# A hybrid encoder layer in float32 on one core: the seven products of the paired down projection in another order, kept sums added later, the gate activation in one call

## The chip, the cores and the metric

The kernel runs on one core of one Trainium2 chip. Its time is the device time of one execution in microseconds (us); lower is better. The time of the kernel before is given as the median of three runs. Beside them stands one profiled execution, from which every duration below is taken.

The engines are named as the profile names them: PE multiplies matrices (PEld is its weight load), DVE (vector), ACT (scalar, activation functions) and POOL (GpSimd) work element by element, SP only issues DMA transfers. ACT and POOL issue some transfers too. SPq is the transfer queue of SP.

## The reference

One layer is applied to two request groups, 256 and 512 tokens of width 1024, all in float32. Three token mixers (a state-space scan, a differential attention and an attention into memory tokens) are gated, merged and projected. The change lies in the last part, the feed-forward network (FFN):

```python
D_FF = -(-8 * D_MODEL // (3 * 256)) * 256          # 2816
    h2 = rmsnorm(x, ffn_norm_g[li])
    g, up = jnp.split(h2 @ w_gate_up[li], 2, axis=-1)
    x = x + (jax.nn.silu(g) * up) @ w_down[li]
```

## The kernel before, in words

**Products.** A float32 product is made of three matmuls: each operand is split into a high part, rounded to the type that PE takes at full speed, and a low part, the rest; high × high, high × low and low × high are summed in PSUM (lines 805 to 807 of `mm3`). The high part is one ACT operation, the low part one DVE subtraction, and the second needs the first.

**The FFN in blocks.** The 768 tokens of both groups are done together. D_FF is cut into 11 blocks of 256 hidden units. For each block there are a gate block and an up block (`block`), from block 1 on each made of seven products of half-size matrices in place of eight (a Strassen–Winograd scheme): four sums of the weights are made on POOL (`_split_w`, lines 581 to 588; each instruction of 128x512), their splits on ACT and DVE (lines 566 and 567), and DVE adds the products in PSUM up into `fs` (line 1514). A block's gate values go to `act_in` (`fa` in the profile) through `fin_gate`: ACT computes t = tanh(c/2) (line 1469), DVE (t + 1) · c (line 1470), which is twice the silu; `fin_up` multiplies the up values in (line 1474). The factor 2 is taken out where these values are split: `left` scales by 0.5.

**The paired down projection.** Blocks 1 and 2, 3 and 4, 5 and 6, 7 and 8 are each taken together after the second block's up (`down_pair`; the text calls this a pair). With A the hidden values (rows: blocks; columns: tokens 0 to 383 and 384 to 767) and B the rows of w_down (columns 0 to 511 and 512 to 1023), the pair is again seven products: A11·B11, S3·T3, S2·T2, A12·B21, S1·T1, A22·T4, S4·B22, in this order, each of 18 matmuls of 128x512 (three token tiles, two steps of k, three matmuls). The left operands A11, A12, A22 are values of `fa`, S1 to S4 are sums on DVE (`left_sum`, tiles `ls`); `left` splits them (ACT line 1552, DVE line 1553; tiles `lS2h`, `lS2l` and so on). The right operands B11, B21, B22 are weights as loaded, T1 to T4 are differences of weights: a tile `wt…x` or `wt…z` is set to a negated one by ACT (`minus`, line 604) and a transfer issued by POOL adds another piece of w_down to it in its memory (`add`, line 603). T3, T2 and T4 are made one after the other in the same tile x: T2 = T3 + B11, T4 = B21 − T2, so T4's transfer waits until T2 is split and negated. `_right` splits each (lines 595 and 596; tiles `wh68_T2`, `wl68_T2`, where 68 is the number of the weight; the profile leaves it out).

**What becomes of the products.** Four of the seven are added by DVE into the rows of the result kept on the chip (`into`, line 1577, tiles `x1` or `x`). The other three, A11·B11, S2·T2 and S1·T1 (`keep` of "1", "6" and "5"), are used by several quarters of the result: ACT copies them out of PSUM (`de`, line 1611), a transfer brings them to DRAM (line 1612), and from the second pair on a transfer issued by POOL adds them to the running sum `p_sum` there (line 1614). `down_sums` reads the three sums back at the end (SP) and adds them with 21 DVE additions (line 1654). It is called before the gate block 9. Blocks 9 and 10 go through `down_last`, plain products, whose results are stored. A product uses three PSUM banks, two of a ring of five and one of a ring of three.

**What sets the order.** Each engine runs its instructions strictly in its own order and waits for other engines by semaphores. A scheduler, which simulates the engines, chooses this order from the program and its dependencies; only transfers in `keep_in_program_order` are pinned to the order of the source. The raw weights come through a ring of three buffers `wr` (half a weight, 512 KB, issued by SP at line 547): the next half can be loaded when the oldest has been split. The split weights lie in rings of four.

Of the kernel before, what the change touches and what calls it, by code (L numbers as in the profile page):

```python
# [507 lines left out]
class WStream:  # L508
# [90 lines left out]
    def _split_d(self, i, h, kind):  # L599
# [6 lines left out]
        if kind == "d" and h == 0:  # L606
            self._right(i, "B11", r)
            self.z = new("z")
            minus(self.z, r)
            add(self.z, b12)  # L610
        elif kind == "d":
            self.x = new("x")
            minus(self.x, r)
            add(self.x, b22)
            self._right(i, "T3", self.x)
        elif h == 0:
            add(self.x, b11)
            self._right(i, "T2", self.x)
            self._right(i, "B21", r)
            self._right(i, "T1", self.z)  # L620
        else:
            minus(self.x, self.x)
            add(self.x, b21)
            self._right(i, "T4", self.x)
            self._right(i, "B22", r)
# [47 lines left out]
def hybrid_block(ctx, tc, A, outs, consts):  # L673
# [792 lines left out]
    def fin_gate(fb, c, m, cs):  # L1466
        n = cs.stop - cs.start
        t = ft_.tile([128, 512], F32, name=uid("ft"), tag="ft")
        act.activation(t[:, 0:n], c, AF.Tanh, scale=0.5)
        v.scalar_tensor_tensor(out=act_in[fb][:, m, cs], in0=t[:, 0:n], scalar=1.0, in1=c, op0=add, op1=mul)  # L1470

    def fin_up(fb, c, m, cs):
        o = act_in[fb][:, m, cs]
        v.tensor_tensor(out=o, in0=o, in1=c, op=mul)
        if fb == 0:
            hh, hl = hid[0]
            act.activation(hh[:, m, cs], o, AF.Copy, scale=0.5)
            v.scalar_tensor_tensor(out=hl[:, m, cs], in0=o, scalar=0.5, in1=hh[:, m, cs].bitcast(F32),
                                   op0=mul, op1=sub)
# [69 lines left out]
    def left(key, src):  # L1549

        hi, lo = (lf.tile([128, 2, HT], F32R, name=uid(f"l{key}{w}"), tag="l" + w) for w in "hl")
        act.activation(hi, src, AF.Copy, scale=0.5)
        v.scalar_tensor_tensor(out=lo, in0=src, scalar=0.5, in1=hi.bitcast(F32), op0=mul, op1=sub)
# [3 lines left out]
    def left_sum(o, x, y, op):  # L1557
        if o is None:
            o = stg.tile([128, 2, HT], F32, name=uid("ls"), tag="brr")
# [3 lines left out]
    def down_begin(fb):  # L1563
# [3 lines left out]
        if fb < NFB - 2:  # L1567
            left("S3", left_sum(None, a[:, :, 0:HT], a[:, :, HT:TOK], sub))
# [22 lines left out]
    def down_pair(fb):  # L1591
# [25 lines left out]
        s1 = left_sum(None, a21, a22, add)  # L1617
        s2 = left_sum(None, s1, a11, sub)
        left("S2", s2)
        into(1, 1, prod("S3", "T3"))  # L1620
        left("A12", a12)
        keep("6", prod("S2", "T2"))
        left("S1", s1)
        into(0, 0, prod("A12", "B21"))
        left("A22", a22)
        keep("5", prod("S1", "T1"))
        left("S4", left_sum(s2, a12, s2, sub))
        into(1, 0, prod("A22", "T4"))
        into(0, 1, prod("S4", "B22"))

    def down_last(fb):
# [3 lines left out]
        for r in range(2):  # L1635
            h = slice(HT * r, HT * r + HT)
            x = [L.pop("A11") if r == 0 else left("A21", a[:, :, h]), left("A2", b[:, :, h])]
            ps = [banks(), banks()]
# [7 lines left out]
    def down_sums():  # L1646

        for t in range(3):
            e = {}
            for key in "165":  # L1650
                e[key] = ft_.tile([128, 512], F32, name=uid("de"), tag="ft")
                nc.sync.dma_start(e[key], p_sum[key][:, t])
            b = {(r, c): out_block(r, c, t) for r in range(2) for c in range(2)}
            plus = lambda o, y: v.tensor_tensor(out=o, in0=o, in1=y, op=add)  # L1654
            plus(b[0, 0], e["1"])
            plus(e["6"], e["1"])
            plus(b[1, 1], e["6"])
            plus(b[1, 0], b[1, 1])
            plus(b[1, 1], e["5"])
            plus(e["6"], e["5"])  # L1660
            plus(b[0, 1], e["6"])
# [214 lines left out]
    for fb in range(1, NFB):  # L1876
        block("gate", fb)
        if fb == NFB - 2:
            down_sums()
# [55 lines left out]
```

## Time and profile before

| | us |
|---|---|
| median of 3 runs (lowest, highest) | 1785.61 (1784.14, 1787.73) |
| the profiled execution's own time | 1783.92 |
| its span, first to last instruction | 1782.1 |
| PE busy in it | 1749.7 (98%) |
| DVE busy | 1309.0 (73%) |
| ACT busy | 910.7 (51%) |
| POOL busy | 251.7 (14%) |

The FFN's first pair begins at 1381.31 us of the span, the last product ends near 1778. In rows of the profile, an instruction in order of time stands as: start, duration, engine, line, operation, output<-inputs, shape; in brackets the idle time of the engine just before it and what ended that. A row of a group has the number of instructions, the busy us, the mean ns, and the idle time before them with what ended most of it. A row of the list of waits is an engine's operation, what it waited for, and then the total us, the number of times and the longest. In tile names the running number is left out, so `wh_T` stands for the high part of T1, T2, T3 or T4.

### The profile page before, as it was taken

The page shows a single profiled execution, that of the slowest core. Times are in us where ns is not written, and L with a number is a line of the kernel's source. Part 1 is how long each engine was busy: PE and PEld are TensorE (multiplying, and loading weights), DVE is VectorE, ACT ScalarE, POOL GpSimd, SP SyncE. Part 2 cuts the span into 40 slices and gives each one's busy share as a digit, 9 for nine tenths or more (in the row PEclk, how much of TensorE's full clock was granted, in tenths as well). Part 3 has the DMA queues.
Part 4 walks back from the last instruction along what each step waited for, and adds up shares of the span by engine and source line. Part 5 has one row for each costly group of instructions (what it writes and reads, how often), then busy time and mean ns, then how long its engine had stood idle before and what let it go on. Part 6 is the DMA issues. An engine that isn't in the chain of part 4 may idle for free. (4 is left out here: it accounts for less than half of the span.)

```text
span 1782.1 us, 29580 instructions
## 1 busy us (share of the span) xinstructions
PE 1749.7 (98%) x11221; PEld 1612.2 (90%) x11221; DVE 1309.0 (73%) x2431; ACT 910.7 (51%) x1894; POOL 251.7 (14%) x283
## 2 busy tenths in 40 slices
PE   8999999999999999999989999999999999999999
PEld 8999988999999998999979888888889898989887
DVE  6665659699999579778875545452699777978795
ACT  6444434877676367778756333232334544444431
POOL 0000000000000101011110101000113333333330
PEclk9999999999999999999999999999999999999999
DMA  7223745664665477454862635332314447474742
GB/s 261 76 84 104 136 113 126 166 166 116 150 151 147 126 182 184 107 113 100 174 165 79 212 122 165 115 100 66 83 48 108 134 109 175 119 174 123 174 128 83
DMA packets 211437, 234.62 MB, mean 132 GB/s; under 512 B 59224, under 2 KB 169056, under 8 KB 211296
## 3 DMA queue, kind: packets, MB, share of 16 engines
q1 hardware_dynamic: 177872, 149.11, 28.4%
q0 software_dynamic: 27088, 71.05, 19.7%
q10 hardware_dynamic: 6336, 12.59, 1.9%
q8 instruction: 88, 1.44, 0.3%
q14 instruction: 53, 0.43, 0.1%
HBM read 163.42 MB, written 49.09 MB: 119 GB/s over the span
## 5 line engine op out<-in xcount | busy, mean ns | idle before, releaser
L641 ACT ACTIVATE wh<-wr 128x1024 fp32r<-128x1024 f32 x130 | 146.6, 1128 | 73.0 <-PE br L806 26.4
L647 DVE TENSOR_TENSOR wl<-wr,wh 128x1024 fp32r<-128x1024 f32 x84 | 110.8, 1320 | 84.1 <-ACT wh L641 82.4
L805 PE MATMUL gl<-Hhi,wh 128*128 128x256 f32 (+1 forms) x384 | 132.3, 344 | 0.0
L807 PE MATMUL gl<-Hhi,wl 128*128 128x256 f32 (+1 forms) x384 | 128.9, 336 | 0.0
L806 PE MATMUL gl<-Hlo,wh 128*128 128x256 f32 (+1 forms) x384 | 128.6, 335 | 0.0
L645 POOL DMA_DIRECT2D wl<-wr x46 | 40.2, 875 | 517.7 <-ACT wl L644 499.7
L805 PE MATMUL qk<-wh,Hhi 128*128 128x256 f32 x384 | 108.6, 283 | 1.6 <-ACT qksq L1232 1.6
L806 PE MATMUL qk<-wl,Hhi 128*128 128x256 f32 x384 | 108.6, 283 | 0.0
L807 PE MATMUL qk<-wh,Hlo 128*128 128x256 f32 x384 | 108.5, 283 | 0.0
L807 PEld LDWEIGHTS gl<-Hhi,wl 128*128 128x128 f32 x384 | 72.0, 188 | 8.0
L806 PEld LDWEIGHTS gl<-Hlo,wh 128*128 128x128 f32 x384 | 72.2, 188 | 7.2
L805 PEld LDWEIGHTS gl<-Hhi,wh 128*128 128x128 f32 x384 | 72.3, 188 | 7.0
L1332 DVE TENSOR_REDUCE nm<-sc 128x1 f32<-128x512 f32 (+1 forms) x96 | 57.1, 597 | 26.6 <-PE sc L1327 25.3
L805 PEld LDWEIGHTS qk<-wh,Hhi 128*128 128x128 f32 x384 | 73.2, 191 | 2.5 <-ACT qksq L1232 1.8
L807 PEld LDWEIGHTS qk<-wh,Hlo 128*128 128x128 f32 x384 | 73.1, 190 | 0.7
L806 PEld LDWEIGHTS qk<-wl,Hhi 128*128 128x128 f32 x384 | 73.1, 190 | 0.5
L567 DVE TENSOR_TENSOR wl_S<-ws,wh_S 128x512 fp32r<-128x512 f32 x70 | 60.5, 884 | 13.5 <-ACT wh_S L566 11.7
L566 ACT ACTIVATE wh_S<-ws 128x512 fp32r<-128x512 f32 x70 | 41.4, 624 | 55.7 <-POOL ws L588 30.4
L1334 ACT ACTIVATE p<-sc,nm 128x512 f32<-128x512 f32 (+1 forms) x96 | 59.0, 616 | 12.5 <-DVE nm L1332 12.0
L1684 ACT ACTIVATE glr<-glr 128x768 f32<-128x768 f32 x24 | 20.3, 846 | 66.2 <-DMA glr<-gl_scr 66.2
L805 PE MATMUL v<-wh,Hhi 128*128 128x256 f32 x192 | 54.1, 282 | 0.0
L806 PE MATMUL v<-wl,Hhi 128*128 128x256 f32 x192 | 54.0, 281 | 0.0
(593 smaller groups left out, 6198.2 us busy)
## 6 DMA issues: line engine op xcount, KB each, us to landing
wr<-in_w_in_dram SPq DMA_DIRECT2D x48, 512.0 KB, 5.1
wl<-wr POOLq DMA_DIRECT2D x46, 512.0 KB, 5.2
wr<-in_w_gate_up_dram SPq DMA_DIRECT2D x44, 512.0 KB, 4.5
wr<-in_w_branch_dram SPq DMA_DIRECT2D x24, 512.0 KB, 4.4
wr<-in_w_down_dram SPq DMA_DIRECT2D x22, 512.0 KB, 4.6
glr<-gl_scr POOLq DMA_DIRECT2D x24, 384.0 KB, 3.6
wr<-in_w_mem_kv_dram SPq DMA_DIRECT2D x16, 512.0 KB, 4.0
wr<-in_w_in_dram SPq DMA_DIRECT2D x32, 256.0 KB, 4.9
```

Of the source, the lines that this page charges most:

```text
L566: self.nc.scalar.activation(f(hi), src, AF.Copy)
L567: self.nc.vector.tensor_tensor(out=f(lo), in0=src, in1=f(hi).bitcast(F32), op=ALU.subtract)
L641: self.nc.scalar.activation(hi, r, AF.Copy)
L645: self.nc.gpsimd.dma_start(lo, r.bitcast(F32R), accum_op=ALU.add)
L647: self.sub.tensor_tensor(out=lo, in0=r, in1=hi.bitcast(F32), op=ALU.subtract)
L805: pe.matmul(ps, wh, xh, start=start, stop=False)
L806: pe.matmul(ps, wh, xl, start=False, stop=False)
L807: pe.matmul(ps, wl, xh, start=False, stop=stop)
L1332: v.tensor_reduce(out=nm[:, m : m + 1], in_=ps, axis=AX.X, op=ALU.max, negate=True)
L1334: act.activation(pm[:, 0:n], ps, AF.Exp, bias=nm[:, m : m + 1], accum_out=s1s[:, tt : tt + 1] if m == 0 else s2)
L1684: act.activation(g, g, AF.Tanh, scale=0.5)
```

## The change

1. The pair's products come in the order A11·B11, S3·T3, A12·B21, S4·B22, S2·T2, S1·T1, A22·T4, and so `keep` of "6" and "5" comes fifth and sixth. The right operands are split in the order B11, T3, B21, T2, B22, T1, T4 (before: B11, T3, T2, B21, T1, T4, B22); T2's negation and T4's transfer are written right after T2's split, before B22 and T1.
2. The sum S4 is written early and has a buffer of its own (tag "do"); before, it was written into S2's buffer.
3. `down_sums` is cut in three, one part for each token tile: the first is called after gate block 10, the two others inside `down_last`, behind its first splits. Its reads are pinned to program order on SP.
4. The gate activation is one ACT operation, Silu, into `act_in`. The values no longer carry the factor 2, and `left` and `fin_up` split without the factor 0.5 (`split_evac`, an existing helper: ACT line 798, DVE line 799). DVE has 2311 instructions where it had 2355 (40 gate operations of 128x384 and four smaller ones are gone), ACT one more (a table load), POOL 263 where it had 259.

```diff
         elif h == 0:
             add(self.x, b11)
+            self._right(i, "B21", r)
+        else:
             self._right(i, "T2", self.x)
-            self._right(i, "B21", r)
-            self._right(i, "T1", self.z)
-        else:
             minus(self.x, self.x)
             add(self.x, b21)
+            self._right(i, "B22", r)
+            self._right(i, "T1", self.z)
             self._right(i, "T4", self.x)
-            self._right(i, "B22", r)
...
     def fin_gate(fb, c, m, cs):
-        n = cs.stop - cs.start
-        t = ft_.tile([128, 512], F32, name=uid("ft"), tag="ft")
-        act.activation(t[:, 0:n], c, AF.Tanh, scale=0.5)
-        v.scalar_tensor_tensor(out=act_in[fb][:, m, cs], in0=t[:, 0:n], scalar=1.0, in1=c, op0=add, op1=mul)
+        act.activation(act_in[fb][:, m, cs], c, AF.Silu)
...
-        act.activation(hi, src, AF.Copy, scale=0.5)
-        v.scalar_tensor_tensor(out=lo, in0=src, scalar=0.5, in1=hi.bitcast(F32), op0=mul, op1=sub)
+        split_evac(hi, lo, src)
...
         keep("1", prod("A11", "B11"))
-        s1 = left_sum(None, a21, a22, add)
-        s2 = left_sum(None, s1, a11, sub)
+        left("A12", a12)
+        s1 = left_sum(a21, a22, add)
+        s2 = left_sum(s1, a11, sub)
+        left("S4", left_sum(a12, s2, sub, "do", 1))
+        into(1, 1, prod("S3", "T3"))
         left("S2", s2)
-        into(1, 1, prod("S3", "T3"))
-        left("A12", a12)
+        into(0, 0, prod("A12", "B21"))
+        left("S1", s1)
+        into(0, 1, prod("S4", "B22"))
+        left("A22", a22)
         keep("6", prod("S2", "T2"))
-        left("S1", s1)
-        into(0, 0, prod("A12", "B21"))
-        left("A22", a22)
         keep("5", prod("S1", "T1"))
-        left("S4", left_sum(s2, a12, s2, sub))
         into(1, 0, prod("A22", "T4"))
-        into(0, 1, prod("S4", "B22"))
...
             x = [L.pop("A11") if r == 0 else left("A21", a[:, :, h]), left("A2", b[:, :, h])]
+            if r == 0:
+                down_sums(1)
+                down_sums(2)
...
         block("gate", fb)
-        if fb == NFB - 2:
-            down_sums()
+        if fb == NFB - 1:
+            down_sums(0)
```

How the scheduler's order differs is shown at three places. The first is ACT in the first pair, from the split of T3 (weights 67 and 68 are those of w_down for blocks 1 and 2). `de` are copies of a kept product, `lS2h`, `lA12h` high parts of left operands, `wt67x` the tile of T3, T2 and T4. Before:

```order
L595 ACTIVATE wh67_T3_15496<-wt67x_15493 128x1024
L595 ACTIVATE wh68_T2_15593<-wt67x_15493 128x1024
L595 ACTIVATE wh68_B21_15597<-wr68_0_15356 128x1024
L604 ACTIVATE wt67x_15493<-wt67x_15493 128x1024
L1611 ACTIVATE de_1647_15689<-dn_1644_15668 128x512
L1612 DMA p_sum1_172<-de_1647_15689 128x512
L1611 ACTIVATE de_1648_15692<-dn_1645_15669 128x512
L1612 DMA p_sum1_172<-de_1648_15692 128x512
L595 ACTIVATE wh68_T1_15601<-wt67z_15488 128x1024
L1611 ACTIVATE de_1649_15695<-dn_1646_15670 128x512
L1552 ACTIVATE lS2h_1652_15702<-ls_1651_15700 128x768
```

And of the changed kernel:

```order
L595 ACTIVATE wh67_T3_15472<-wt67x_15469 128x1024
L595 ACTIVATE wh68_B21_15569<-wr68_0_15340 128x1024
L595 ACTIVATE wh68_T2_15575<-wt67x_15469 128x1024
L1604 ACTIVATE de_1635_15665<-dn_1632_15644 128x512
L1605 DMA p_sum1_172<-de_1635_15665 128x512
L1604 ACTIVATE de_1636_15668<-dn_1633_15645 128x512
L604 ACTIVATE wt67x_15469<-wt67x_15469 128x1024
L1605 DMA p_sum1_172<-de_1636_15668 128x512
L798 ACTIVATE lA12h_1638_15674<-fa_1608_15309 128x768
```

The split of B21 now stands ahead of that of T2, and the third product's left operand (now A12) comes five instructions and issues after T2's split, where the third one's before (S2) came nine after it. On DVE the same pair has, behind T2's low part, these rows in the changed kernel (`fs` and `fa` are the up block's sums and the hidden values, `ls` the sums of left operands; before, the low parts of B21 and T1 and the additions of an `into` stood there ahead of S2's low part):

```order
L596 TENSOR_TENSOR wl68_T2_15576<-wt67x_15469,wh68_T2_15575 128x1024
L1471 TENSOR_TENSOR fa_1608_15309<-fa_1608_15309,fs_1624_15479 128x384
L1553 TENSOR_TENSOR ls_1641_15680<-ls_1640_15678,fa_1589_15032 128x768
L1553 TENSOR_TENSOR ls_1642_15682<-fa_1608_15309,ls_1641_15680 128x768
L799 TENSOR_TENSOR lA12l_1639_15675<-fa_1608_15309,lA12h_1638_15674 128x768
```

Here the low part of A12 stands four places behind that of T2, with the sums for S2 and S4 between them.

The second place is POOL in the second pair (weights 73 and 74), from the transfer for T1 on. `wt73x<-in_w_down` are the transfers for T3, T2 and T4 in this order, `ws75…` the sums for the next gate block's weight. Before:

```order
L603 DMA wt73z_16324<-in_w_down_dram 128x2x512
L603 DMA wt73x_16329<-in_w_down_dram 128x2x512
L588 TENSOR_TENSOR ws723_16172<-wr72_1_16025,ws721_16170 128x512
L603 DMA wt73x_16329<-in_w_down_dram 128x2x512 x2
L1614 DMA p_sum1_172<-p_scr_1740_16525 128x512
L581 TENSOR_TENSOR ws750_16476<-wr75_0_16336,wr75_1_16441 128x512
```

Of the changed kernel:

```order
L603 DMA wt73z_16285<-in_w_down_dram 128x2x512
L603 DMA wt73x_16290<-in_w_down_dram 128x2x512
L588 TENSOR_TENSOR ws723_16141<-wr72_1_15994,ws721_16139 128x512
L603 DMA wt73x_16290<-in_w_down_dram 128x2x512
L581 TENSOR_TENSOR ws750_16437<-wr75_0_16297,wr75_1_16394 128x512
L582 TENSOR_TENSOR ws751_16438<-ws750_16437,wr75_0_16297 128x512
L586 TENSOR_TENSOR ws752_16439<-wr75_0_16297 128x512
L1607 DMA p_sum1_172<-p_scr_1721_16486 128x512
L603 DMA wt73x_16290<-in_w_down_dram 128x2x512
```

T4's transfer, the last row, stood right behind T2's; it now stands behind three sums of the next weight and one transfer of a kept product.

The third place is DVE at the end of the program. Before, the last of the 21 additions stood in the gate block 10, ahead of its last two gate operations:

```order
L1654 TENSOR_TENSOR x1_5_12337<-x1_5_12337,de_1996_18599 128x512
L1654 TENSOR_TENSOR x1_2_12334<-x1_2_12334,de_1995_18597 128x512
L647 TENSOR_TENSOR wl91_1_18904<-wr91_1_18748,wh91_1_18903 128x1024
L1470 SCALAR_TENSOR_TENSOR fa_2006_18747<-ft_2017_18873,fs_2007_18780 128x384
L1470 SCALAR_TENSOR_TENSOR fa_2006_18747<-ft_2019_18890,fs_2008_18781 128x384
```

Of the changed kernel (`dn` is a product of the last projection, `x1_0` to `x1_5` rows of the result, `de` the sums that were read back):

```order
L1570 TENSOR_TENSOR x1_0_12332<-x1_0_12332,dn_1993_18940 128x512
L1650 TENSOR_TENSOR x1_5_12337<-x1_5_12337 128x512
L1650 TENSOR_TENSOR de_1991_18929<-de_1991_18929,de_1992_18931 128x512
L1570 TENSOR_TENSOR x1_1_12333<-x1_1_12333,dn_1994_18941 128x512
L1570 TENSOR_TENSOR x1_2_12334<-x1_2_12334,dn_1995_18942 128x512
L1650 TENSOR_TENSOR x1_5_12337<-x1_5_12337,de_1992_18931 128x512
L1650 TENSOR_TENSOR x1_2_12334<-x1_2_12334,de_1991_18929 128x512
```

The last additions of kept sums now stand between the additions that take the last projection's products out of PSUM; the first seven stand in the up block 10.

More of the change, by code (lines that the diff above doesn't have):

```diff
@@ L1476, in fin_up @@
             hh, hl = hid[0]
-            act.activation(hh[:, m, cs], o, AF.Copy, scale=0.5)
-            v.scalar_tensor_tensor(out=hl[:, m, cs], in0=o, scalar=0.5, in1=hh[:, m, cs].bitcast(F32),
-                                   op0=mul, op1=sub)
+            split_evac(hh[:, m, cs], hl[:, m, cs], o)
     def new_block(what, fb):
@@ L1551, in left, with left_sum @@
         hi, lo = (lf.tile([128, 2, HT], F32R, name=uid(f"l{key}{w}"), tag="l" + w) for w in "hl")
-        act.activation(hi, src, AF.Copy, scale=0.5)
-        v.scalar_tensor_tensor(out=lo, in0=src, scalar=0.5, in1=hi.bitcast(F32), op0=mul, op1=sub)
+        split_evac(hi, lo, src)
         L[key] = hi, lo
         return hi, lo
-    def left_sum(o, x, y, op):
-        if o is None:
-            o = stg.tile([128, 2, HT], F32, name=uid("ls"), tag="brr")
+    def left_sum(x, y, op, tag="brr", bufs=2):
+        o = stg.tile([128, 2, HT], F32, name=uid("ls"), tag=tag, bufs=bufs)
         v.tensor_tensor(out=o, in0=x, in1=y, op=op)
@@ L1567, in down_begin @@
         if fb < NFB - 2:
-            left("S3", left_sum(None, a[:, :, 0:HT], a[:, :, HT:TOK], sub))
+            left("S3", left_sum(a[:, :, 0:HT], a[:, :, HT:TOK], sub))
     def out_block(r, c, t):
@@ L1644, in down_last, with down_sums @@
                 into(r, c, ps[c], done=True)
[L1646 to L1661, printed above, removed]
+    def down_sums(t):
+        e = {}
+        for key in "165":
+            e[key] = ft_.tile([128, 512], F32, name=uid("de"), tag="ft")
+            tc.keep_in_program_order(nc.sync.dma_start(e[key], p_sum[key][:, t]))
+        b = {(r, c): out_block(r, c, t) for r in range(2) for c in range(2)}
+        plus = lambda o, y: v.tensor_tensor(out=o, in0=o, in1=y, op=add)
+        plus(b[0, 0], e["1"])
+        plus(e["6"], e["1"])
+        plus(b[1, 1], e["6"])
+        plus(b[1, 0], b[1, 1])
+        plus(b[1, 1], e["5"])
+        plus(e["6"], e["5"])
+        plus(b[0, 1], e["6"])
     with ExitStack() as c5:
```

## The prediction

> **What bounds the kernel now.** I read the page's first part, then the waits of TensorE from 1190 us to the end, then PE, ACT and DVE in order of time around the longest wait. First the page, and the list of waits (engine, line, what ended the wait: total us, times, longest):
>
> ```profile
> PE 1749.7 (98%) x11221; PEld 1612.2 (90%) x11221; DVE 1309.0 (73%) x2431; ACT 910.7 (51%) x1894; POOL 251.7 (14%) x283
> PE dn L805 <- ACT lS2h L1552: 6.8, 3, 2.9
> PE gate L805 <- DVE fs L1514: 2.8, 3, 1.6
> PE up L805 <- DVE fs L1514: 0.8, 1, 0.8
> ```
>
> PE is the bound, and the change takes no product away. So only PE's idle time and its clock can be gained. Everything ahead of the FFN keeps its order on every engine. In the FFN 6.8 us go to the product S2·T2 of three of the four paired down projections (pairs, below), and 2.8 + 0.8 = 3.6 us to the gate and up blocks. The next fence is PE in order of time, then windows (length, busy us of PE, PEld, DVE, ACT, POOL, granted clock, DMA share, GB/s):
>
> ```profile
> 1379.23 0.33 PE L805 MATMUL up<-fhi,wh_S 128*128 128x384 f32 x1
> ...
> 1381.31 0.39 PE L805 MATMUL dn<-wh_B,lA11h 128*128 128x512 f32 x1
> ...
> 1389.28 0.39 PE L807 MATMUL dn<-wh_T,lS3l 128*128 128x512 f32 x1
> 1392.57 0.50 PE L805 MATMUL dn<-wh_T,lS2h 128*128 128x512 f32 x1 [2.90 <-ACT lS2h L1552]
> 1571.42 0.78 PE L805 MATMUL dn<-wh_T,lS2h 128*128 128x512 f32 x1 [2.87 <-ACT lS2h L1552]
> 1661.24 0.50 PE L805 MATMUL dn<-wh_T,lS2h 128*128 128x512 f32 x1 [1.03 <-ACT lS2h L1552]
> 1717.87 0.41 PE L805 MATMUL gate<-T2h,wh_S 128*128 128x384 f32 x1 [1.58 <-DVE fs L1514]
> 1394.10:1397.50 3.40, 3.40 (x10) 2.67 (x9) 3.40 (x5) 0.49 (x1) 0.00 (x0) 0.52 0.92 275
> 1571.40:1575.00 3.60, 3.58 (x9) 2.84 (x10) 3.60 (x7) 1.44 (x2) 0.00 (x0) 0.53 1.07 276
> 1661.00:1664.40 3.40, 3.16 (x14) 2.63 (x15) 3.40 (x6) 1.65 (x3) 0.01 (x1) 1.00 1.07 267
> ```
>
> Two products are 36 matmuls: 35 steps in 1389.28 - 1381.31 = 7.97 us, so 4.1 us a product; the last product of the up block takes 1381.31 - 1379.23 = 2.1. After the two waits of 2.9 us the clock stands at about half; after 1.03 and 1.58 us it does not fall. The half clock costs 3.40 × 0.48 + 3.60 × 0.47 = 3.3 us more. At stake are 6.8 + 3.3 + 3.6 = **13.7 us**.
>
> Why S2 is late: ACT, then DVE, in order of time in the first pair.
>
> ```profile
> 1384.89 1.06 ACT L595 ACTIVATE wh_T<-wt67x 128x1024 fp32r<-128x1024 f32 x1 [10.50 <-DMA wt67x<-in_w_down_dram]
> 1387.24 1.06 ACT L604 ACTIVATE wt67x<-wt67x 128x1024 f32<-128x1024 f32 x1 [0.34 <-DVE wl_T L596]
> 1391.69 0.83 ACT L1552 ACTIVATE lS2h<-ls 128x768 fp32r<-128x768 f32 x1
> 1397.01 1.06 ACT L595 ACTIVATE wh_T<-wt67x 128x1024 fp32r<-128x1024 f32 x1 [3.02 <-DMA wt67x<-in_w_down_dram]
> 1385.98 1.22 DVE L596 TENSOR_TENSOR wl_T<-wt67x,wh_T 128x1024 fp32r<-128x1024 f32 x1 [4.11 <-ACT wh_T L595]
> 1390.18 0.96 DVE L1560 TENSOR_TENSOR ls<-ls,fa 128x768 f32<-128x768 f32 x1
> ```
>
> T2's transfer lands at 1384.89. ACT and DVE both stand in their order before its split, and the sums for S2 are queued behind. S2's high part ends at 1391.69 + 0.83 = 1392.52, 7.6 us after T2 has landed; PE takes it at 1392.57.
>
> **The change part by part.**
>
> *Order of the products.* The third product is now A12·B21, and S2·T2 the fifth, 8.2 us later, so S2 cannot be the wait. But A12's high part stands behind the split of T2 on ACT, and its low part behind it on DVE. Its lateness from T2's landing is a sum of durations (groups: count | busy us, mean ns):
>
> ```profile
> L1611 ACT ACTIVATE de<-dn 128x512 f32<-128x512 f32 x36 | 20.9, 587 | 3.7 <-PE dn L807 1.8 <-ACT de L1611 1.7
> L1552 ACT ACTIVATE lA12h<-fa 128x768 fp32r<-128x768 f32 x4 | 3.3, 833 | 0.0
> L1553 DVE SCALAR_TENSOR_TENSOR lA12l<-fa,lA12h 128x768 fp32r<-128x768 f32 x4 | 3.8, 951 | 0.0
> ```
>
> ACT: split of T2 1.0, an eviction with its DMA issue 1.0, another 0.6, the negation 1.0 (DVE's 1.22 has ended by then), a DMA issue 0.3, A12 0.83: 4.7 us, so A12 is there at 1384.89 + 4.7 = 1389.6. PE is ready for the third product at 1389.28 + 0.23 = 1389.5. DVE: 1.06 + 1.22, the gate product 0.5, two sums of 0.95 and then A12's low part, 0.95 after the high one: 5.7 us, against a need six matmuls later, 4.6 + 1.4 = 6.0. So the 2.9 us come down to about nothing, with no slack; in the third pair, where the wait was equal, the same; the fourth (1.03) and the second (no wait) have room.
>
> What moves T2's landing or that chain is new neighbours. B21 is now split before T2, so the raw half of the next gate weight that takes its buffer is loaded some 6 to 9 us earlier, into T2's transfer, and the three POOL sums that wait for it run beside the DVE chain. The nearest rows are in the second pair, POOL, DVE, ACT and SP:
>
> ```profile
> 1477.41 1.20 POOL L603 DMA_DIRECT2D wt73x<-in_w_down_dram  x1 [8.88 <-ACT wt73x L604]
> 1488.39 1.29 POOL L581 TENSOR_TENSOR ws<-wr,wr 128x512 f32<-128x512 f32 x1 [7.23 <-DMA wr<-in_w_gate_up_dram]
> 1490.23 1.53 POOL L582 TENSOR_TENSOR ws<-ws,wr 128x512 f32<-128x512 f32 x1
> 1491.63 1.38 POOL L586 TENSOR_TENSOR ws<-wr 128x512 f32<-128x512 f32 x1
> 1488.78 1.72 DVE L1553 SCALAR_TENSOR_TENSOR lA22l<-fa,lA22h 128x768 fp32r<-128x768 f32 x1 [1.00 <-ACT lA22h L1552]
> 1491.02 3.08 DVE L596 TENSOR_TENSOR wl_B<-wr,wh_B 128x1024 fp32r<-128x1024 f32 x1
> 1485.41 1.06 ACT L595 ACTIVATE wh_T<-wt73x 128x1024 fp32r<-128x1024 f32 x1 [2.61 <-DMA wt73x<-in_w_down_dram]
> 1478.51 0.37 SPq L547 DMA_DIRECT2D wr<-in_w_gate_up_dram  x1
> wr<-in_w_gate_up_dram SPq DMA_DIRECT2D x44, 512.0 KB, 4.5
> ```
>
> T4's transfer, issued at 1477.41 beside that load, took 8.0 us; the load 1488.39 - 1478.51 = 9.9, against a median of 4.5. Beside the three sums (4.2 us) two DVE operations took 0.77 and 1.86 us over their usual 0.95 and 1.22, 2.6 us in all. So a T2 later by 0 to 2 us and a chain later by 0 to 2.6, in two pairs: 0 to 9.2 us, and 3.3 of half clock at the upper end. The load meets only the tail of T2's transfer, and the sums start when it has landed, when half the chain is past; I take **+1.0 in each of two pairs, +2.0 us**.
>
> *T4.* The source moves it up; on POOL it moves back, behind those three sums and, from the second pair on, one more DMA issue (1.2). Counted from a pair's start (its first product): B21's buffer is free when the up block has two products left, -4.2; its split on ACT and DVE, with three DVE sums ahead, ends near -1, and the load is issued. I take 5.5 for the load (4.5 and a meeting with T2's tail), 4.2 for the sums, 1.2, and 8.0 for T4: landed at +17.9, where the row above has 1397.01 - 1381.31 = +15.7. The seventh product wants T4 at 6 × 4.1 = +24.6. But on DVE three evictions of the fourth product stand behind T4's split, and the sixth product wants their banks from 5 × 4.1 + 2.7 = +23.2. Landing, both splits (1.06 + 1.22) and two evictions (0.6 each) make +21.4: 1.8 us to spare, so nothing; R3 is its bound.
>
> *Gate activation.* One ACTIVATE of the same shape stays on ACT, and a DVE operation goes, 40 times and 4 smaller ones:
>
> ```profile
> L1470 DVE SCALAR_TENSOR_TENSOR fa<-ft,fs 128x384 f32<-128x384 f32 x40 | 29.5, 742 | 6.9 <-ACT ft L1469 5.9
> L1469 ACT ACTIVATE ft<-fs 128x384 f32<-128x384 f32 x40 | 20.8, 522 | 47.7 <-DVE fs L1514 42.8 <-DVE fa L1470 3.8 <-DVE de L1654 1.0
> L641 ACT ACT_TABLE_LOAD x1 | 1.3, 1283 | 0.7 <-PEq L1918 0.7
> ```
>
> 29.5 us of DVE are off PE's path and pay only where PE waited for DVE. I take the new function at tanh's 522 ns (no row has it; same input and output). One table load more stands at the first call, 0 to 1.3 us; PE has other products there: +0.3. The Trainium skill (ScalarE: Activation LUTs, What ACT_TABLE_LOAD costs) puts a switch with its drain at 2.66 us; by that page the term would be at most 2.7, and no run here shows the drain. Splitting unscaled copies (one subtraction for a scaled one) costs and gains nothing: 768 elements take 0.95 either way.
>
> *Kept sums.* 21 DVE additions leave the last two gate/up blocks before PE's last products; 7 now come beside the last up block, 14 beside the last projection.
>
> ```profile
> L1654 DVE TENSOR_TENSOR x<-x,de 128x512 f32<-128x512 f32 x12 | 7.8, 680 | 0.0
> L1654 DVE TENSOR_TENSOR de<-de,de 128x512 f32<-128x512 f32 x6 | 4.2, 704 | 0.0
> de<-p_sum SPq DMA_DIRECT2D x9, 256.0 KB, 2.8
> 1756.74 0.69 DVE L1577 TENSOR_TENSOR x<-x,dn 128x512 f32<-128x512 f32 x1 [1.56 <-PE dn L807]
> 1771.25 0.69 DVE L1577 TENSOR_TENSOR x<-x,dn 128x512 f32<-128x512 f32 x1 [8.83 <-PE dn L807]
> ```
>
> They total 14 us with the three other additions. The 3.6 us of waits lay beside them, and DVE stood idle 8.8 us under the last products, so they have cover. In-order waits on their loads (2.8 us, two or three of them) now stand ahead of the up block's evictions and of the first six stores' additions: 0 to 3 us; the banks leave about 5. I take **+0.4**.
>
> Sum: -13.7 + 2.0 + 0.3 + 0.4 = **-11.0 us**. The profiled execution took 1783.92 (span 1782.1), 1.7 below the median of the runs, and becomes 1772.9; the median, 1785.61, becomes **1774.6 us**.
>
> **Rivals.**
>
> *R1, the neighbours hold A12.* POOL sums and the early load put the full 2.6 us on the third product in pairs 1 and 3: with half clock 2 × (2.6 + 1.65) = 8.5 in place of 2.0, so 1774.6 + 6.5 = 1781.1. For it: the missing slack. Against: gate operations of 742 ns leave DVE ahead of T3's split, so T2 may start sooner. The Trainium skill (SBUF — State Buffer, Who interferes with whom) has a rule against this change: GpSimd and a VectorE operation with two SBUF inputs exclude each other for a whole instruction. By it all 4.2 us of sums could fall on the chain; the trace agrees in kind, with 2.6 us of 4.2. By that page two pairs would lose 2 × (4.2 + 1.65) = 11.7 in place of 2.0, an estimate of 1784.3.
>
> *R2, the wait only changes place.* T2's landing stays what it was, another operand behind it waits, in all pairs, with the half clock: about 1785. Against it is the shorter queue, 4.7 for 7.6 us.
>
> *R3, slower: T4 holds the evictions.* If the load ahead of the POOL sums takes 9.9 instead of 5.5 us, T4 lands 4.4 later than counted, 2.6 beyond the spare time. PE then stops in the sixth product of every pair, long enough for half clock: 4 × (2.6 + 1.65) = 17 us, time 1774.6 + 17 = 1791.6. With half clock a stop of 11.0 / 4 - 1.65 = 1.1 us a pair already takes the whole gain. Against it: in that row the load ran beside T4's own transfer, which now comes after it.
>
> **How the numbers follow.** Forecast 0.58, R1 0.17, R2 0.12, R3 0.13. A measurement of this kernel tells 0.2%, 3.6 us, from no change, so faster means below 1782.0: the forecast and two thirds of R1, 0.69. Same: a third of R1 and R2, 0.18. Slower: R3, 0.13. The range goes from all waits gone and no new one (1771.9) less the runs' spread, 1770.0, to 1785.0: the forecast, R1 and about half of R2, some 0.8.
>
> **What would show it.** Right: no half clock inside the pairs; waits of PE on lA12h below 1.5 us in two pairs and none on lS2h; no wait on fs in the last two blocks; T4 landing some 5 us later and unnoticed. Wrong: waits on lA12 near 3 us with clock 0.5 behind them (R1, R2); PE waiting for x in the sixth product (R3); waits on fs or x beside the last projection (the kept sums).

## The result

| | us |
|---|---|
| before, median of 5 runs (lowest, highest) | 1785.61 (1784.04, 1787.73) |
| changed, median of 5 runs (lowest, highest) | 1769.18 (1765.31, 1770.34) |
| ratio changed / before, 95% interval | 0.9901 (0.9888, 0.9914) |

The changed kernel is 16.4 us faster. The forecast was 11.0 us faster, and the range, 1770.0 to 1785.0, misses the median by 0.8 us. The direction and the places were right; the gain was too small by a third.

Of the changed kernel, first the page's row of the engines, then PE's list of waits from 1190 us to the end (engine and line, what ended the wait: total us, times, longest):

```profile
PE 1744.7 (99%) x11221; PEld 1611.2 (91%) x11221; DVE 1278.9 (72%) x2387; ACT 913.6 (52%) x1895; POOL 250.8 (14%) x283
```

```profile
PE gate L805 <- DVE x L1540: 0.7, 1, 0.7
PE nT L834 <- DVE flo L799: 0.5, 1, 0.5
PE gate L806 <- DVE flo L799: 0.2, 1, 0.2
PE dn L805 <- DVE x L1540: 0.2, 1, 0.2
```

Nothing is left of the waits on `lS2h` and on `fs`. What remains lies in the first two blocks and was there before in other places (1.6 us, before 1.7). By the page DVE has 44 instructions fewer than before (2387 for 2431), ACT one more, and POOL as many (283).

For the account by stages I read the start of the first matmul of each stage (the FFN's first gate matmul starts at 1266.91 us in both profiles, by accident: on the way there they are up to 2.2 us apart, each with one stretch of half clock, at 677 us before and at 13 us after):

| stage | before | changed | difference |
|---|---|---|---|
| FFN's first gate matmul to the first pair | 114.40 | 114.28 | -0.12 |
| pair 1 | 33.43 | 28.60 | -4.83 |
| pair 2 | 28.91 | 28.60 | -0.31 |
| pair 3 | 33.39 | 28.60 | -4.79 |
| pair 4 | 29.93 | 28.60 | -1.33 |
| the three stretches of gate and up blocks between the pairs | 174.81 | 174.79 | -0.02 |
| blocks 9 and 10, last projection, to PE's end | 96.23 | 91.11 | -5.12 |
| PE's end to the span's end | 4.11 | 4.10 | -0.01 |

The sum is -16.5 us, the difference of the two spans (1782.1 and 1765.6). 28.60 us are 126 matmuls at 0.227 us: a pair now runs without a stop. In order of time on PE, the third product of pair 1 after the change:

```profile
1389.16 0.39 PE L807 MATMUL dn<-wh_T,lS3l 128*128 128x512 f32 x1
1389.39 0.39 PE L805 MATMUL dn<-wh_B,lA12h 128*128 128x512 f32 x1
...
1390.52 0.39 PE L806 MATMUL dn<-wl_B,lA12h 128*128 128x512 f32 x1
1390.75 0.39 PE L807 MATMUL dn<-wh_B,lA12l 128*128 128x512 f32 x1
```

There is no bracket and so no idle time ahead of A12's high part (`lA12h`) nor, six matmuls on, ahead of its low part.

### The profile page after: what moved, and what is told of

Its sections match the earlier page's. It is cut to its first block, busy times and chain, and to the rows that moved or that the text cites. A ratio compares the mean times of both kernels' runs of the same rounds, so it can differ in the third digit from the quotient of the medians.

```text
span 1765.6 us, 29522 instructions
## 1 busy us (share of the span) xinstructions
PE 1744.7 (99%) x11221; PEld 1611.2 (91%) x11221; DVE 1278.9 (72%) x2387; ACT 913.6 (52%) x1895; POOL 250.8 (14%) x283
## 4 chain that ended last, share of the span: by engine, by line
PE 91%; DVE 3%; DMA 3%; ACT 1%; issue 1%; SPq 1%; POOL 0%; DVEq 0%; ACTq 0%; POOLq 0%
PE gl L805 4%; PE gl L807 4%; PE gl L806 4%; PE br L806 4%; PE br L805 4%; PE br L807 4%; PE up L805 3%; PE up L806 3%; PE up L807 3%; PE gate L806 3%; PE gate L807 3%; PE gate L805 3%; PE dn L805 3%; PE dn L807 3%; PE dn L806 3%; PE av L1363 2%
## 5 line engine op out<-in xcount | busy, mean ns | idle before, releaser
L567 DVE TENSOR_TENSOR wl_S<-ws,wh_S 128x512 fp32r<-128x512 f32 x70 | 54.5, 801 | 25.3 <-ACT wh_S L566 24.7
L1334 ACT ACTIVATE p<-sc,nm 128x512 f32<-128x512 f32 (+1 forms) x96 | 59.1, 617 | 13.6 <-DVE nm L1332 13.2
L1509 DVE TENSOR_TENSOR fs<-fs,up 128x384 f32<-128x384 f32 x70 | 37.4, 548 | 24.4 <-PE up L807 23.5
L1680 ACT ACTIVATE glr<-glr 128x768 f32<-128x768 f32 x24 | 20.3, 847 | 65.7 <-DMA glr<-gl_scr 64.4
```

The costliest lines, as they stand in the source:

```text
L567: self.nc.vector.tensor_tensor(out=f(lo), in0=src, in1=f(hi).bitcast(F32), op=ALU.subtract)
L1334: act.activation(pm[:, 0:n], ps, AF.Exp, bias=nm[:, m : m + 1], accum_out=s1s[:, tt : tt + 1] if m == 0 else s2)
L1509: v.tensor_tensor(out=o, in0=x, in1=y, op=add)
```

## The experiments

The change has three parts that can be done apart: the order of the products with its splits and buffer (**order**), the Silu with the unscaled splits (**Silu**), the moved additions (**sums**). Each was tried alone, and each was left out alone. The theories: **A**, the Silu moves T2's landing forward, and the order by itself has no slack; **B**, the order by itself removes the waits. The stages are read as above; "loss" is what the four pairs take over 4 × 28.60 us.

| kernel | ratio to before (95%) | pairs 1, 2, 3, 4 | loss | blocks 9, 10 to PE's end |
|---|---|---|---|---|
| before | 1 | 33.43, 28.91, 33.39, 29.93 | 11.3 | 96.23 |
| order alone | 0.9945 (0.9926, 0.9964) | 32.06, 28.60, 28.60, 28.60 | 3.5 | 93.61 |
| Silu alone | 0.9998 (0.9986, 1.001) | 28.62, 28.72, 28.71, 28.89 | 0.5 | 103.69 |
| sums alone | 0.9977 (0.9963, 0.999) | 33.05, 29.02, 33.18, 29.87 | 10.7 | 91.11 |
| order and sums, no Silu | 0.9929 (0.9911, 0.9948) | 33.41, 28.60, 28.60, 28.60 | 4.8 | 91.11 |
| Silu and sums, old order | 0.9914 (0.9898, 0.993) | 28.63, 28.62, 28.99, 28.93 | 0.8 | 91.11 |
| order and Silu, old sums | 0.9979 (0.997, 0.9989) | 28.60, 28.60, 28.60, 28.60 | 0 | 101.71 |
| all three | 0.9901 (0.9888, 0.9914) | 28.60, 28.60, 28.60, 28.60 | 0 | 91.11 |

### The order alone

```diff
         elif h == 0:
             add(self.x, b11)
+            self._right(i, "B21", r)
+        else:
             self._right(i, "T2", self.x)
...
+        into(0, 0, prod("A12", "B21"))
+        left("S1", s1)
+        into(0, 1, prod("S4", "B22"))
+        left("A22", a22)
         keep("6", prod("S2", "T2"))
```

> Alone on the kernel before: the new order of the pair's products with its operand splits and S4's buffer; tanh gate and kept sums as before. The two profiles at hand put T2's landing 3.4 us earlier in the changed kernel (1381.52 against 1384.89) and DVE 3.1 us longer over the operations beside POOL's three sums. Theory A (the landing came forward because of the gate activation, the order alone has no slack): T2 lands near 1384.9, A12's low part is ready near 1384.9 + 5.7 + 3.1 = 1393.7 against a need at 1390.9, so the first and third pair still lose 2 to 3 us each to A12, with or without half clock: gain 2 to 6 us. Theory B (the order is what removes the waits): no wait in any pair, gain the pairs' 11.4 us (4.87 + 0.35 + 4.83 + 1.36 over the seamless 28.6). Both: the 5.2 us lost in the last two blocks stay.

Measured: 0.9945, some 10 us; by the profile's stages 7.8 us in the pairs and 2.6 us in the last blocks, where no gain was expected. PE's waits from 1260 us on:

```profile
PE dn L807 <- DVE lA12l L1553: 2.2, 1, 2.2
PE dn L805 <- DVE x L1545: 1.0, 1, 1.0
PE up L805 <- DVE fs L1514: 0.8, 1, 0.8
PE dn L805 <- ACT lA12h L1552: 0.6, 1, 0.6
```

Pair 1 does as theory A says, it waits for A12's low part; pairs 2 to 4 do as B says. T2's transfer lands 4.1 us after the first product's start in pair 1, and 0.3 us after it in pair 3, where before it was 3.5 us. The order of the products is the same in both pairs, and the one where T2 still lands late keeps its wait: it is the landing that decides, as in theory A, though in pair 3 it comes forward without the Silu. By the trace the loads of w_down for pair 3 go out 26.1 us ahead of its start, where before it was 22.7; why the new order brings them forward by itself was not followed further.

### The Silu alone

```diff
-        act.activation(t[:, 0:n], c, AF.Tanh, scale=0.5)
-        v.scalar_tensor_tensor(out=act_in[fb][:, m, cs], in0=t[:, 0:n], scalar=1.0, in1=c, op0=add, op1=mul)
+        act.activation(act_in[fb][:, m, cs], c, AF.Silu)
```

> Alone on the kernel before: the gate activation as one Silu and the unscaled splits; products and kept sums as before. Theory A: T2 lands 2.9 to 3.4 us earlier in the first and third pair, S2's high part with it, and its wait of 2.9 us and the half clock go: gain 9 to 11 us in the pairs. Theory B: S2 keeps its place nine instructions behind T2's split, the waits shrink by less than 1 us each, half clock stays: gain under 3 us in the pairs. In the last two blocks: if their waits came from the gate operations on DVE, 5.2 us go with them; if from the 21 additions, they stay.

Measured: no difference (0.9998), and two large ones inside. The loss in the pairs is 0.5 us with the old order, as theory A says. But blocks 9 and 10 take 103.69 us, 7.5 more than before. (Its profiled execution was the shortest of its twelve, 1778.70 us against a median of 1784.17: the trace gives the places, the ratio the worth.) First ACT and POOL in order of time around pair 1, whose first matmul starts at 1379.41 us in this run; behind the dots DVE and PE in gate block 9:

```profile
1373.76 1.20 POOL L603 DMA_DIRECT2D wt67x<-in_w_down_dram  x1 [10.09 <-DVE wl_T L596]
...
1379.78 1.06 ACT L595 ACTIVATE wh_T<-wt67x 128x1024 fp32r<-128x1024 f32 x1 [7.60 <-DMA wt67x<-in_w_down_dram]
1386.58 0.84 ACT L798 ACTIVATE lS2h<-ls 128x768 fp32r<-128x768 f32 x1
...
1676.69 1.17 DVE L1648 TENSOR_TENSOR x<-x,de 128x512 f32<-128x512 f32 x1 [9.66 <-DMA de<-p_sum]
1681.68 0.69 PE L805 MATMUL gate<-T1h,wh_S 128*128 128x384 f32 x1 [6.10 <-DVE x L1571]
```

T2's transfer is issued 5.7 us ahead of the pair's first matmul (before: 1381.31 - 1378.40 = 2.9) and its split starts 0.4 us behind it (before: 3.6). S2's high part ends at 1387.42, 8.0 us after the pair's start, where two products end at 8.2. The old order is quick enough then. In gate block 9 an addition of a kept sum (`x<-x,de`) stands on DVE ahead of the additions that empty PE's banks (`x L1571`); DVE idles 9.7 us for its read, and PE stops for 6.1. The first read is issued 5.1 us ahead of gate block 9 here (1664.04), and 20.3 us behind its start in the kernel before (1702.04).

### The moved sums alone

```diff
-        if fb == NFB - 2:
-            down_sums()
+        if fb == NFB - 1:
+            down_sums(0)
```

(with `down_sums(1)` and `down_sums(2)` in `down_last`).

> Alone on the kernel before: the 21 additions of kept sums moved to the last up block and the last projection. The pairs keep all their waits (2.90, 2.87, 1.03). If the additions caused the waits of the last two blocks, the whole 5.2 us lost there go (3.6 us of listed waits and some 0.27 a stop): 1780.4 by the median. If the two-part gate activation caused them, less than 2 us go. If the reads of the sums stall DVE in the last projection, a wait on x appears there.

Measured: 0.9977, 4.1 us less by the ratio; the pairs nearly as before, and the last stretch 91.11 us, all of the 5.1. So the additions caused the waits of the last blocks, not the gate operations, and their new place costs PE nothing.

### All but the Silu

The order and the sums, with the tanh and the scaled splits of the kernel before.

> The changed kernel with the tanh gate and scaled splits put back. Theory A: waits on A12 of 2 to 3 us in the first and third pair, 5 to 9 us slower than the changed kernel. Theory B: within 2 us of the changed kernel (1769.2), since the order and the moved sums are there.

Measured: 0.9929 (0.9911, 0.9948), against 0.9901 (0.9888, 0.9914) with the Silu: 5.0 us by the ratios, only 1.9 by the medians (1771.12 and 1769.18, measured at different times), and the intervals touch. The times alone do not tell the two theories apart; the trace does: A's wait is there in pair 1, and not in pair 3, where A expected it too. In pair 1, DVE and POOL in order of time:

```profile
1388.93 1.65 DVE L1474 TENSOR_TENSOR fa<-fa,fs 128x384 f32<-128x384 f32 x1
1390.62 1.93 DVE L1559 TENSOR_TENSOR ls<-ls,fa 128x768 f32<-128x768 f32 x1
1392.58 1.91 DVE L1559 TENSOR_TENSOR ls<-fa,ls 128x768 f32<-128x768 f32 x1
1394.42 0.94 DVE L1553 SCALAR_TENSOR_TENSOR lA12l<-fa,lA12h 128x768 fp32r<-128x768 f32 x1
...
1388.14 2.03 POOL L581 TENSOR_TENSOR ws<-wr,wr 128x512 f32<-128x512 f32 x1 [7.08 <-DMA wr<-in_w_gate_up_dram]
1390.25 1.49 POOL L582 TENSOR_TENSOR ws<-ws,wr 128x512 f32<-128x512 f32 x1
1391.69 1.99 POOL L586 TENSOR_TENSOR ws<-wr 128x512 f32<-128x512 f32 x1
```

Three DVE operations that take 0.55, 0.95 and 0.95 us elsewhere take 1.65, 1.93 and 1.91 beside POOL's three sums: 3.0 us late, and PE waits 0.34 for A12's high part and 2.25 for its low part. Pair 1 loses 4.8 us, with the half clock behind it. That is rival R1 of the prediction, at the predicted price (2.6 us of waits and 1.65 of half clock, the rest is what two stops cost besides), in one pair instead of two. T2 lands 3.8 us after the start of pair 1 in this run, and 0.5 after that of pair 3.

### POOL's sums behind T4's transfer

The same kernel, with T4's transfer and the first sum of the next weight pinned in the program's order on POOL:

```diff
-        gt(out=s1, in0=A21, in1=A22, op=add)
+        self.pin(gt(out=s1, in0=A21, in1=A22, op=add))
...
-            add(self.x, b21)
+            self.pin(add(self.x, b21))
```

> The changed kernel without the Silu (as the run of that name, whose first pair lost 4.8 us, 2.25 of it in a wait for A12's low part), and on POOL T4's transfer pinned ahead of the next weight's sums in the pairs. The transfer waits for the negation, so the sums start about 3 us later, behind most of the DVE operations that lead to A12's low part. If POOL's sums lengthen those (1.65, 1.93 and 1.91 us for 0.55, 0.95 and 0.95), they fall back to these, A12's low part comes 2 to 3 us earlier, and the first pair takes at most 29.3 us. If the lateness of T2's landing is the cause, the wait of 2.2 us stays.

Measured (a single run, 1772.95 us): pair 1 takes 30.47 us, not 33.41, and not the 29.3 expected. DVE and POOL there:

```profile
1391.23 0.55 DVE L1475 TENSOR_TENSOR fa<-fa,fs 128x384 f32<-128x384 f32 x1
1391.82 0.96 DVE L1560 TENSOR_TENSOR ls<-ls,fa 128x768 f32<-128x768 f32 x1
1392.81 0.96 DVE L1560 TENSOR_TENSOR ls<-fa,ls 128x768 f32<-128x768 f32 x1
1393.69 2.45 DVE L1554 SCALAR_TENSOR_TENSOR lA12l<-fa,lA12h 128x768 fp32r<-128x768 f32 x1
...
1393.53 1.78 POOL L582 TENSOR_TENSOR ws<-wr,wr 128x512 f32<-128x512 f32 x1
```

The three operations are back at 0.55, 0.96 and 0.96. Now the first sum falls on A12's low part itself, which takes 2.45 us for 0.95. So POOL's sums do lengthen DVE's operations, and moving the sums moves the delay: the wait on `lA12l` fell from 2.2 to 1.2 us, and the clock stayed full. Without the 1.5 us the low part would have ended at 1394.64, ahead of 1394.95, where PE wanted it: this wait is the sum's. T2 lands 4.0 us after the pair's start in this run too, which leaves A12 0.3 us of room. It takes both to make the wait: in the changed kernel, where T2 lands at 0.3 us, a lengthening of 3.1 us costs PE nothing.

### The old order with Silu and sums

All of the change but the order of the products, the splits and S4's buffer.

> The changed kernel with the old order of the pair's products, splits and buffer put back (the Silu and the moved sums stay). In the trace of the Silu alone the four pairs took 28.62, 28.72, 28.71 and 28.89 us against 28.60 in the changed kernel, and in that of the moved sums alone the last two blocks and the projection behind them 91.11. If the parts add, the pairs together are 0.5 us longer than in the changed kernel and the rest equal: the order is then worth 0.5 us where the Silu is there. If the order is needed, waits on lS2h of more than 1 us come back.

Measured: 0.9914 (0.9898, 0.993), the same as the whole change within the intervals; the pairs take 0.8 us more than in the changed kernel (0.5 expected), with no listed wait in them. Beside the Silu, the order is worth 0.8 us by the trace, which these runs cannot tell from nothing.

### The old sums with order and Silu

> The changed kernel with the 21 additions back before gate block 9. The kept products 6 and 5 now leave the pair as its fifth and sixth, later than before, so the sums in memory are ready later. If the 6.1 us stop of the Silu-alone run came from an addition on DVE standing in its order ahead of what frees PE's banks, while its read waits for the last pair's accumulation, a stop of at least 6 us comes here too at the beginning of gate block 9, and the part from there to PE's end is over 100 us (91.1 in the changed kernel). If that stop was an accident of the old product order, it stays below 95.

Here `down_sums` is again called whole, as in the kernel before. (In the source that call stands behind `block("gate", 9)`, not ahead of it, as the text ahead of the prediction and the expectation say; where its instructions then stand is the scheduler's choice.) Measured: 0.9979, and 101.71 us from gate block 9 to PE's end, 10.6 more than in the changed kernel. It is the stop of the Silu-alone run, though in another place: not PE's banks at the beginning of block 9 but the sums `fs` of the block. DVE and PE in order of time:

```profile
1679.96 0.69 DVE L1647 TENSOR_TENSOR x<-x,de 128x512 f32<-128x512 f32 x1 [6.38 <-DMA de<-p_sum]
1690.52 0.69 DVE L1647 TENSOR_TENSOR x<-x,de 128x512 f32<-128x512 f32 x1 [3.88 <-DMA de<-p_sum]
...
1696.62 0.66 PE L805 MATMUL up<-fhi,wh_A 128*128 128x384 f32 x1 [5.74 <-DVE fs L1509]
```

DVE idles 6.4 and 3.9 us for reads of the kept sums, and PE then stops for 5.7 us at the up block. The first read is issued at 1675.66, 1.6 us behind gate block 9's start. The source has a reason why the reads go so early with the Silu: the tanh's results, the copies of kept products and the sums that are read back share a ring of three buffers (tag "ft"). With the tanh, its results of gate block 9 stand in that ring ahead of the reads; with the Silu nothing of the block does, and the reads run into the last pair's accumulations, of which the last lands at 1681.29 in the Silu-alone run and at 1686.07 in this one. This was read from the source and the rows; no run took the ring alone.

With the Silu the moved sums are worth 10.6 to 12.6 us (101.71 and 103.69 against 91.11), without it 5.1 and 2.5 us (96.23 and 93.61 against 91.11).

### A known delay of A12

The changed kernel, with A12's high part written three times in place of once:

```diff
+        for _ in range(late):
+            act.activation(hi, src, AF.Copy)
         split_evac(hi, lo, src)
...
-        left("A12", a12)
+        left("A12", a12, 2)
```

> The changed kernel with A12's high part written three times instead of once (two more ACT operations of 0.84 us, behind which S4's high part and others come in between): by the changed kernel's trace it is there at 1391.1 instead of 1386.4, where PE wants it at 1389.4. One wait of about 1.6 us in each pair. If a stop costs what the list of waits shows, a pair takes 28.60 + 1.6 = 30.2 us; if 0.27 us more (restart of PE), 30.5. If the clock falls by the share of a fixed window of 3.41 us in which PE is busy (below about 0.45 in the traces so far), it does not fall here, since 1.75 us leave 0.49 at the worst.

Measured (a single run, 1776.31 us): pairs of 30.73, 29.46, 30.49 and 30.49 us. The stop in pair 1 in order of time on PE:

```profile
1391.32 0.39 PE L807 MATMUL dn<-wh_T,lS3l 128*128 128x512 f32 x1
1393.54 0.50 PE L805 MATMUL dn<-wh_B,lA12h 128*128 128x512 f32 x1 [1.83 <-ACT lA12h L798]
1393.87 0.39 PE L806 MATMUL dn<-wl_B,lA12h 128*128 128x512 f32 x1
```

The waits are 1.83, 0.56, 1.58 and 1.58 us (in pair 2 A12 had more room than the expectation from pair 1), and the pairs take 2.13, 0.86, 1.89 and 1.89 more than 28.60: each stop costs 0.30 us beyond the idle time listed. The rows show where: from the matmul before the stop to the one behind it pass 2.22 us, where 0.23 is a step, so 1.99 for 1.83 listed; and the next step takes 0.33, 0.11 more. The clock stayed full in all four; the lowest busy share of a window was 62%.

**What the runs say together.** Each theory holds in part. Either the order or the Silu takes most of the pairs' waits away, and where a wait goes, T2 has come to land earlier. Over the nine kernels without the added delay of A12 the landing sorts the pairs: where T2 lands 3.1 to 4.1 us after the start, the pair loses 1.9 to 4.8 us, in the old order and in the new; at 1.6 us 1.3; at up to 0.8 us at most 0.4 in the old order and nothing in the new. The Silu brings the landing forward in all pairs that were late, the order in pairs 3 and 4; pair 1 needs the Silu. The moved sums take away the waits of the last blocks, and the Silu needs them. In the whole change the pairs are without a stop and the last stretch is at the 91.11 us of three other kernels, so in these stages PE has no listed idle time left.

## Why the prediction was right or wrong

**What was at stake was too small.** The first step that failed is the price of a stop. The prediction counted 6.8 + 3.3 + 3.6 = 13.7 us: listed waits, and the half clock. The stages gave 16.5. The difference is the restart of PE, 0.30 us a stop as the run with the known delay shows: 1.2 us for four stops in the pairs (pair 2 stopped too: 0.02 us of idle time, 0.31 of loss) and 1.5 for five in the last blocks (5.12 against 3.6; 0.11 of it is the idle time of the fifth, which does not appear in the list). It stood in the rows that the prediction quotes: 1392.57 - 1389.28 is 3.29 us from matmul to matmul, which less a step of 0.23 is 3.06, not 2.90. The range failed by the same term: its lower end was built on 1785.6 - 13.7 = 1771.9 for all waits gone; with 16.5 that is 1769.1, and 1769.18 was measured.

**The order of the products: right in the chain, wrong in its start.** The chain from T2's split to A12 held, and POOL's sums lengthened it (by 3.1 us, a little over the bound of 2.6). The other step that failed is "its lateness from T2's landing", counted from T2's landing as it was, and 0 to 2 us later. That holds only for pair 1 without the Silu (T2 0.3 to 0.6 us later, and a pair that loses 3.5 to 4.8 us). In the whole change T2 came earlier, in pair 3 as in pair 1 (0.2 and 0.3 us after the start, before 3.5). The changed kernel, ACT and DVE in order of time in pair 1:

```profile
1372.89 1.06 ACT L595 ACTIVATE wh_T<-wt67x 128x1024 fp32r<-128x1024 f32 x1 [2.02 <-PE up L806]
1381.52 1.06 ACT L595 ACTIVATE wh_T<-wt67x 128x1024 fp32r<-128x1024 f32 x1 [3.41 <-DMA wt67x<-in_w_down_dram]
...
1385.59 0.84 ACT L798 ACTIVATE lA12h<-fa 128x768 fp32r<-128x768 f32 x1
```

```profile
1383.88 1.64 DVE L1471 TENSOR_TENSOR fa<-fa,fs 128x384 f32<-128x384 f32 x1
1385.56 1.94 DVE L1553 TENSOR_TENSOR ls<-ls,fa 128x768 f32<-128x768 f32 x1
1387.53 1.93 DVE L1553 TENSOR_TENSOR ls<-fa,ls 128x768 f32<-128x768 f32 x1
1389.38 0.94 DVE L799 TENSOR_TENSOR lA12l<-fa,lA12h 128x768 fp32r<-128x768 f32 x1
```

T2 is split at 1381.52 instead of 1384.89, 3.4 us earlier. The DVE operations lose their 3.1 us beside POOL's sums all the same, and A12's low part still ends at 1390.32, ahead of 1390.75 where PE takes it. So the residual of +2.0 us was none, and R1 did not decide. Without the Silu it does, in pair 1.

The prediction had the reason in hand, as an argument against R1 ("gate operations of 742 ns leave DVE ahead of T3's split, so T2 may start sooner"), and put no number on it. The Silu-alone run shows it: T2's transfer went out 2.7 us earlier against the pair's start (5.65 for 2.91), with the old order. The rows say where. T2's transfer waits for T3's low part on DVE. Before, ACT, DVE and POOL in order of time:

```profile
1373.34 1.05 ACT L595 ACTIVATE wh_T<-wt67x 128x1024 fp32r<-128x1024 f32 x1
1376.88 1.22 DVE L596 TENSOR_TENSOR wl_T<-wt67x,wh_T 128x1024 fp32r<-128x1024 f32 x1
1378.40 1.20 POOL L603 DMA_DIRECT2D wt67x<-in_w_down_dram  x1 [10.85 <-DVE wl_T L596]
```

Of the changed kernel, DVE and POOL:

```profile
1373.99 1.23 DVE L596 TENSOR_TENSOR wl_T<-wt67x,wh_T 128x1024 fp32r<-128x1024 f32 x1
1375.51 1.20 POOL L603 DMA_DIRECT2D wt67x<-in_w_down_dram  x1 [10.12 <-DVE wl_T L596]
```

Before, T3's high part was done at 1374.39, and DVE came to the low part 2.5 us later; in the changed kernel it comes as soon as the high part is done (1373.95). DVE works without a listed idle time ahead of it in both: before from 1364.66 us on, with three gate operations of 0.55 us among its work, now from 1362.48 on with none. T3's high part itself moved by only 0.45 us, though the loads of w_down go out at 1355.28 instead of 1357.36: it now waits for a buffer that an up product releases (the 2.02 us in the first row above). So T2 can hardly come earlier still: in none of the forty pairs of the ten traces does its transfer go out more than 5.7 us ahead of the pair. That DVE's queue carries the shift was read from the rows, and no run took it alone.

By the rule that the prediction cited from the Trainium skill (SBUF — State Buffer, Who interferes with whom), GpSimd and a VectorE operation with two SBUF inputs take turns for a whole instruction. The pinned run agrees in kind: the operations are at full speed when no sum runs, and the one beside a sum took 1.5 us more. But not all 4.8 us of the sums came on top, 3.1 did.

**T4: right, unnoticed.** It landed 13.6, 19.0, 17.5 and 16.6 us after the start of pairs 1 to 4 where +17.9 was forecast, and the sixth product never waited. "Some 5 us later" was 6.7, 2.3 and 3.6 us later in pairs 2 to 4 and 2.1 earlier in pair 1. The bound of R3, 1.8 us later than forecast, was not reached.

**The gate activation.** The new function takes what tanh took: 516 ns in the mean for 40 calls of the same shape (522 before), and the table load 1.28 us, which PE does not show (the stretch that holds it became 0.12 us shorter). The forecast of 0.3 for it was nothing. Its worth was not in what it frees beside PE's waits, where the forecast sought it, but in T2.

**Kept sums: right, at no cost.** The forecast of +0.4 was 0. One read held DVE 1.3 us, under the last products. The sums-alone run shows that the waits on `fs` were theirs. What the prediction did not see is that they are needed: with the Silu and the old call, blocks 9 and 10 would have lost 10.6 us. The forecast added up three parts as if they were apart; by the FFN's stages they give 10.4, 3.4 and 5.7 us alone (the Silu's from its shortest run, and nothing by its ratio), 19.5 in sum, and 16.5 together: in the pairs two of them cure the same waits, and in the last blocks the Silu costs 7.5 where the sums stay.

**R2**, that the wait only changes place, did not happen in the whole change. In part it happened in the order-alone run, in pair 1.

So -11.0 lacks 5.5 us: 2.8 at stake that were not counted (2.7 of it the nine stops: their restarts, and 0.1 us of idle time that the list leaves out), 2.0 for A12 that T2's earlier landing paid, and 0.7 for the table and the sums.

## What to carry to other kernels

Read what a stop costs from one matmul's start to the next, less a step, and not from the idle time listed: here 0.30 us a stop were missing, a sixth of the gain. When a change takes work off an engine in one place, follow which buffer becomes free sooner and which transfer starts sooner, before the lateness of another place is counted from where it was. Parts that cure the same wait do not add (order 7.8 and Silu 10.7 us of the pairs' 11.3), and a part that makes work earlier can run into a transfer that has not landed: try each alone and left out.

## What the runs showed of the hardware

**The clock is judged in fixed windows.** Each stretch of half clock inside the program is 3.41 us long, or two such in a row, and within one run they begin whole multiples of 3.413 us apart (sums alone: 676.6, 901.9, 922.4, 1396.8 and 1574.3 us, 66, 72, 211 and 263 of them after the first). In these traces it goes with PE's busy share in the window before. The rows are windows of the order-alone run and then of the run with all but the Silu, each cut to these limits (length, busy us of PE, PEld, DVE, ACT, POOL, granted clock, DMA share, GB/s):

```profile
1389.80:1393.20 3.40, 1.66 (x6) 1.05 (x6) 3.37 (x3) 1.78 (x4) 3.40 (x3) 1.00 0.00 0
1393.20:1396.60 3.40, 2.71 (x12) 2.26 (x13) 3.40 (x5) 2.33 (x3) 0.08 (x1) 1.00 0.76 164
```

```profile
1392.90:1396.30 3.40, 1.15 (x6) 0.75 (x5) 3.40 (x4) 1.77 (x3) 1.93 (x2) 0.99 0.14 26
1396.30:1399.70 3.40, 3.40 (x10) 2.62 (x9) 3.40 (x5) 0.76 (x1) 0.00 (x0) 0.50 1.10 251
```

In both runs pair 1 stops twice for A12, 0.63 and 2.24 us in the first, 0.34 and 2.25 in the second. The longer sum left PE busy 1.66 of 3.40 us in one window, and the clock stayed full; the shorter one, lying otherwise to the windows, left 1.15, and the next window ran at half. Through the FFN of all ten traces, up to PE's last matmul, the nine windows in which PE was busy up to 42% were followed by half clock, and those from 49% on were not; none lies between. The prediction's reading, that 2.9 us trigger it and 1.58 do not, was too simple: a stop of some 2 to 3 us pays 1.6 us more or not by where it falls. The Trainium skill (TensorE: Matmul & The Clock Gate, The HAM clock gate) has these windows: 3413 ns, free-running, the throttle after an idle one. The traces agree in the length and in the free run; the window need not be idle, 42% busy was not enough.

**Part of the spread between runs goes with it.** Up to the FFN's first gate matmul PE's order is the same in all these kernels, and yet that matmul starts between 1265.12 and 1270.73 us: at 1265.12 in the run with no stretch of half clock before it, at 1266.91 in the two with one, and at 1269.08 to 1270.73 in the four with three. The three runs with two of them lie at 1266.61, 1268.41 and 1270.58, so it is not the only cause, and no run tested it.

**A stop costs 0.30 us beyond its idle time**, for stops of 0.56 to 1.83 us alike: about 0.16 before the first matmul and 0.11 behind it; where the last 0.03 lie was not found.
